# Load order at the end of attention, and the order of loads and forms in the output projection, of a one-core encoder block

## The chip, the cores and the metric

The kernel runs on one core of a Trainium2 chip. The metric is device time in microseconds (us) of one execution, as the median of several runs. Five engines work side by side and are ordered by semaphores: TensorE (PE in the profile; PEld is its weight load), VectorE (DVE), ScalarE (ACT), GpSimd (POOL) and SyncE (SP). SP computes nothing here: it issues nearly all DMA transfers, one behind the other, from one queue.

## The reference, cut to what matters

One residual block on x of 512 tokens by 2048 features, all in float32:

```python
h = rmsnorm(x, g_attn)
proj = h @ w_in                        # q, k, v of 8 + 8 heads of 128, and 8 forget gates
o_sb = stick_breaking_attention(...)   # 8 heads
o_fox = forgetting_attention(...)      # 8 heads
mixed = concat(head_rmsnorm(o_sb), head_rmsnorm(o_fox))
x = x + mixed @ w_out
u = relu(rmsnorm(x, g_mlp) @ w_up)
x = x + (u * u) @ w_down
y = rmsnorm(x, g_final)
```

The change touches the last head of the attention and `x + mixed @ w_out`, the output projection.

## The kernel before, in words

**Precision.** Every float32 operand of a matmul is split in two float32r parts, a high half (a cast, on ScalarE) and a low half (the operand less its high half, on VectorE). A product is three matmuls: high by high, high by low, low by high (`mm3`, lines 78 to 80). In names, `wh`, `wl` are the halves of a weight piece and `g`, `f` those of a left operand. A weight piece is 2 row blocks by 512 columns and takes 12 matmuls (2 token blocks x 2 row blocks x 3).

**The projection as seven products.** `mixed @ w_out` is computed in 2 x 2 blocks with seven block products instead of eight (numbered 1, 5, 6, 3, 7, 4 and 2), once for each of two column halves, `db` 0 and 1. Each product p needs a left *form* of the blocks of mixed: `a_source` (line 1329) makes it with one subtraction or addition on VectorE for 5, 6, 7 and 3, in place, so that the form of 6 is built on that of 5 and that of 3 on that of 6. `g_form(p, (m0, m1), ...)` (line 1498) makes the forms for row blocks m0 to m1 and splits them (cast on ScalarE, low half on VectorE). The right sides are sums of blocks of w_out that were made and stored in device memory during the attention (`wsums`, `whigh`, `wraws`).

**Product 2 comes early.** It needs only heads that are finished early (the forgetting heads). So its four pieces for each column half stand in the schedule of the attention's last step, n = 16, at the time `t` = 16 steps. The class `Second` (line 1136 on) loads a piece (`load_parts` for half 0, both halves from `wraws`, line 1146; `load` for half 1, raw), and multiplies it. The pieces go in the order m0 = 4, 6, 0, 2. The pieces 4, 6 and 0 take the next tiles of a ring of three (`hi_lo`, line 69); piece 2 has tiles of its own.

**Who sets the order.** In the attention a `Plan` collects jobs with times and emits them sorted by time. TensorE, ScalarE and VectorE run them in exactly that order. For SP this holds only up to the job `free_loads` (line 1280); behind that a planner orders SP's transfers by a simulation of its own, in which an earlier place in the program means a higher priority. In the output projection no order is written by hand: the planner places all engines, and `tc.issue_after(ins)` only says that what is traced inside it must come behind `ins` on the engine of `ins`.

**The transpose.** The weights of each head but the last are turned by a DMA: `halves` (ScalarE copies the 16-bit halves apart, line 941) at 24.7 us of a step and `turn_halves` (line 945, a `dma_start_transpose` on SP) at 24.8 us. The steps are 26.05 us long, so for head 14 these stand at t - 1.35 and t - 1.25 of step 16. The turned weights are joined (line 949), split (`ph` line 953, `pl` line 956) and multiplied with v (`product` of head 14, output tile `o`).

**The loop of the projection** (line 1623) goes over the products and the four pieces m0 = 0, 2, 4, 6 of each. `out_piece` loads, splits and multiplies a piece and returns the load. Behind a piece the loop may
- turn a finished quarter of the residual stream (`turn_quarter`, line 1567: eight transposes on TensorE into two PSUM buffers, four scaled copies on ScalarE into the tile `hr[db][j]`, and a store); column half 1 uses the same buffers for `hr[1][j]` as half 0 for `hr[0][j]`,
- make one pending left form for the up projection (`left_form`, line 1588) from `hr[0][j]`, behind the last cast and the last low half so far,
- begin a quarter (`begin`, line 1543: a load of x of 512 KB), to which `take` (line 1547) adds the product,
- make forms of mixed for a later product (the table `G_AT`, line 1594).

Piece (6, 4) means m0 = 4 of product 6.

Of the kernel before, what the change touches and what calls it, by code (L numbers as in the profile page):

```python
# [38 lines left out]
def block_kernel(ctx, tc, x, g_attn, w_in, b_f, g_out_sb, g_out_fox, w_out, g_mlp, w_up, w_down, g_final, y):  # L39
# [16 lines left out]
    lows, last_heads = [None], [None] * 7  # L56
# [165 lines left out]
    with ExitStack() as stage:  # L222
# [23 lines left out]
        plan = Plan()  # L246
# [82 lines left out]
        for k in range(2, K8):  # L329
            if k < 6:  # L330
                room[k] = early_w[0][:, 4:6] if k == 2 else early_w[1][:, 2 * k - 6:2 * k - 4]
                w = Placed(room[k])
            else:
                w = Piece(w_rows[k][:, :, c0:c0 + m], 2, m)
# [41 lines left out]
        for k in range(4, K8):  # L376
            t, j = mm_at[k], k + K8
            w = pieces[k][0]
# [387 lines left out]
    with tc.tile_pool(name="att", bufs=1, side="right", reuse_waits="tile") as at, \  # L766
# [9 lines left out]
        plan = Plan()  # L776
# [403 lines left out]
        for n in range(2 * NH + 1):  # L1180
            t = TPER * n
# [33 lines left out]
            else:  # L1215
# [4 lines left out]
                for db in range(2):  # L1220
                    for n0, m0 in enumerate((4, 6, 0, 2)):
                        w = Second(db, m0)
                        if db:
                            plan.at(t + (-10.0, -9.0, -8.0, 6.0)[n0], w.load)
                            plan.at(t + (3.4, 4.5, 10.3, 11.35)[n0], w.cast_apart if n0 < 2 else w.cast, *((n0,) if n0 < 2 else ()))
                            plan.at(t + (4.6, 7.0, 11.75, 12.95)[n0], w.low)
                        else:
                            plan.at(t + (-11.0, -5.5, 0.1, -1.4)[n0], w.load_parts)
                        for tt in range(2):
                            plan.at(t + at_unit16(unit), w.multiply, tt)  # L1230
                            unit += 1
# [266 lines left out]
    def g_form(p, *parts):  # L1498
        for m0, m1 in parts:
            a_form(p, mixed_halves[:, m0:m1], [g[:, m0:m1, :] for g in G[p]])  # L1500
# [90 lines left out]
        a_form(p, hr[db][j], [F[p][db][:, 2 * j:2 * j + 2, c, :] for c in range(2)])  # L1591

    pending, to_turn = [], []
    G_AT = {(5, 6): (3, (0, 4), (4, 6)), (6, 0): (3, (6, 8)), (6, 2): (7, (0, 4)), (6, 4): (7, (4, 6)), (6, 6): (7, (6, 8))}
    for db in range(2):
        quarter[0, 0] = second_x[db]
        if db == 1:
            pending += [(1, 0, j) for j in (1, 0)]
        else:

            g_form(1, (0, 4), (4, 6))
            with tc.issue_after(last_heads[2].ins):
                g_form(4, (0, 4), (4, 8))
            with tc.issue_after(last_heads[5].ins):
                g_form(5, (0, 4), (4, 6))
            more_parts.append(lambda: parts_at(px, "px"))
            with tc.issue_after(last_heads[3].ins):
                out_piece(1, 0, 0)
            with tc.issue_after(last_heads[0].ins):
                out_piece(1, 0, 2)  # L1610
                out_piece(1, 0, 4)
            begin(1, 0, 0)
            with tc.issue_after(last_heads[1].ins):
                for m0 in (0, 2, 4, 6):
                    ins = out_piece(4, 0, m0)
            for p in (1, 5):
                g_form(p, (6, 7), (7, 8))
            take(4, 0)
            with tc.issue_after(ins.ins):
                begin(1, 1, 0)  # L1620
            with tc.issue_after(last_heads[6].ins):
                g_form(6, (0, 4), (4, 6), (6, 8))
        for p in (1, 5, 6, 3, 7, 4)[:6 if db else 5]:
            for m0 in () if db == 0 and p == 1 else (0, 2, 4, 6):
                if db == 0 and p == 5 and m0 == 6:
                    out_piece(1, 0, 6)
                    take(1, 0)
                    last_heads[4] = taken[0]
                    to_turn += [(0, 0, 0)]
                ins = out_piece(p, db, m0)  # L1630
                if m0 in (0, 2) and to_turn:
                    with tc.issue_after(ins.ins):
                        turn_quarter(*to_turn.pop(0))
                    if db == 1 and p == 4:
                        left_form(1, 1, 1)
                        for j in range(2):
                            left_form(2, 1, j)
                        for q in (4, 5, 6):
                            left_form(q, 1, 1)
                if pending:  # L1640

                    with tc.issue_after(casts[0].ins), tc.issue_after(lows[0].ins):
                        left_form(*pending.pop(0))
                if (db or p in (3, 7, 4)) and m0 in (2, 6) and first_loads:

                    with tc.issue_after(ins.ins):
                        u, k, a = first_loads.pop(0)
                        units[u].load(k, a)
                if db == 0 and p == 5 and m0 == 6:

                    with tc.issue_after(ins.ins):
                        begin(0, 1, db)
                if db == 0 and (p, m0) in G_AT:

                    with tc.issue_after(last_heads[4].ins):
                        g_form(*G_AT[p, m0])
            if db == 0 and p == 6:
                more_parts.pop()
                px_cm.__exit__(None, None, None)
# [8 lines left out]
            if db == 1 or p != 1:  # L1668
                take(p, db)
            if db == 1:  # L1670
                pending += [(q, 0, j) for j in range(2) for q in {1: (4, 5, 6), 6: (2, 7, 3)}.get(p, ())]
            if len(squares) > 0:

                with ExitStack() as order_:
# [596 lines left out]
```

## Time and profile before

| | |
|---|---|
| median of 3 runs | 2011.31 us (2009.68 to 2012.33) |
| the profiled execution, its own time | 2010.09 us |
| its span, from the first to the last instruction | 2008.3 us |
| granted TensorE clock over the span | 0.998 |
| TensorE busy | 1992.1 us |
| VectorE busy | 1754.1 us |
| ScalarE busy | 1204.9 us |
| GpSimd busy | 63.4 us |

How to read the profile. A line of the timeline gives the start and the length in us, the engine, the line of the kernel, the operation, output<-inputs, the shape, and the count of merged instructions. In brackets stands how long the engine was idle before it and what ended that. `SPq` lines are transfers being issued on SP's queue: their length is the issue, not the transfer. A matmul's length is its latency; they follow each other sooner than that. A row of the waits gives who waited for whom, the total in us, how often, and the longest. A row of windows gives the stretch, its length, busy time of PE, PEld, DVE, ACT and POOL with counts, the granted clock, the mean share of the DMA engines and GB/s.

By stage, from windows of 20 us: TensorE is busy for all of nearly every window. It is short of 20 us from 580 to 600 (15.58), 640 to 660 (18.77), 660 to 680 (19.69), 720 to 740 (19.66), 760 to 780 (18.90), 780 to 800 (19.95), and at the end, from 2000 on. The last step of the attention begins at about 585, the output projection lies between about 614 and 757, the up projection begins at 757.

### The profile page before, as it was taken

To read this page: it belongs to the slowest core of one execution; us is meant where nothing else is said; L and a number is where in the kernel's file an instruction comes from. 1 tells how busy PE (TensorE), PEld (TensorE's weight loads), DVE (VectorE), ACT (ScalarE), POOL (GpSimd) and SP (SyncE) were. 2 spreads that over 40 slices of the span, in tenths; PEclk is the share of its full clock that TensorE was granted. 3 is DMA by queue.
4 is the path that set the end of the run, shared out by engine and by line. 5 is a ranking of instruction groups with operands and counts; after the bars stand their busy time and mean duration, and the time that the engine had idled before them with its cause. 6 is when DMAs were issued, how large, how long until landed. Compare 5 with 4: busy or idle time off the path is not lost.

```text
span 2008.3 us, 26668 instructions
## 1 busy us (share of the span) xinstructions
PE 1992.1 (99%) x10096; PEld 1709.8 (85%) x10096; DVE 1754.1 (87%) x1992; ACT 1204.9 (60%) x1636; POOL 63.4 (3%) x73
## 2 busy tenths in 40 slices
PE   9999999999999999999999999999999999999998
PEld 9988888888878789888888888888888888888887
DVE  8876888888887688999999999998798888988896
ACT  7544666677874565767676766766543444444444
POOL 0000011111010000000000000000000000000003
PEclk9999999999999999999999999999999999999999
DMA  7336977677786872566666665666795674674642
GB/s 263 125 139 212 283 240 238 201 218 231 225 264 230 305 238 95 182 206 208 204 189 215 190 222 189 210 202 234 251 328 173 234 269 154 234 268 166 215 164 85
DMA packets 309072, 426.66 MB, mean 212 GB/s; under 512 B 49440, under 2 KB 198736, under 8 KB 302416
## 3 DMA queue, kind: packets, MB, share of 16 engines
q1 hardware_dynamic: 307920, 422.33, 63.7%
q10 hardware_dynamic: 1024, 2.63, 0.3%
q8 instruction: 79, 1.29, 0.2%
q14 instruction: 49, 0.40, 0.1%
HBM read 318.07 MB, written 97.01 MB: 207 GB/s over the span
## 4 chain that ended last, share of the span: by engine, by line
PE 95%; DVE 2%; DMA 1%; ACT 1%; issue 0%; DVEq 0%; SPq 0%; ACTq 0%
PE psa L1415 11%; PE accd L80 8%; PE accd L78 8%; PE accd L79 8%; PE accq L78 6%; PE accq L80 6%; PE accq L79 6%; PE psa L1413 6%; PE psc L1415 5%; PE psc L1413 3%; PE psb L1415 3%; PE psb L1413 1%; PE m L80 1%; PE m L78 1%; PE m L79 1%; PE vy L79 1%
## 5 line engine op out<-in xcount | busy, mean ns | idle before, releaser
L2057 ACT CAST wh<-wd 128x1024 fp32r<-128x1024 f32 x126 | 124.9, 998 | 168.8 <-PE accd L80 54.6
L1943 DVE TENSOR_TENSOR wl<-wu,wh 128x1024 fp32r<-128x1024 f32 x157 | 191.4, 1220 | 13.5 <-ACT wh L1937 13.4
L78 PE MATMUL accq<-hH,wh 128*128 128x512 f32 x512 | 200.3, 391 | 0.0
L79 PE MATMUL accq<-hL,wh 128*128 128x512 f32 x512 | 199.4, 389 | 0.0
L80 PE MATMUL accq<-hH,wl 128*128 128x512 f32 x512 | 199.3, 389 | 0.0
L1937 ACT CAST wh<-wu 128x1024 fp32r<-128x1024 f32 x157 | 166.4, 1060 | 48.7 <-PE psc L1415 25.7
L1415 PE MATMUL psa<-f,wh 128*128 128x512 f32 x712 | 177.1, 391 | 0.0
L79 PE MATMUL accd<-wl,uf 128*128 128x512 f32 x436 | 169.6, 389 | 0.0
L80 PE MATMUL accd<-wh,uf 128*128 128x512 f32 x436 | 169.6, 389 | 0.0
L78 PE MATMUL accd<-wh,uf 128*128 128x512 f32 x436 | 169.4, 389 | 0.0
L2064 DVE TENSOR_TENSOR wl<-wd,wh 128x1024 fp32r<-128x1024 f32 x126 | 144.0, 1152 | 11.5 <-ACT wh L2057 11.5
L1415 PEld LDWEIGHTS psa<-f,wh 128*128 128x128 f32 x712 | 130.8, 188 | 25.3
L2057 ACT CAST wx<-wd 128x1024 fp32r<-128x1024 f32 (+1 forms) x82 | 80.8, 995 | 106.8 <-PE accd L80 42.9
L1778 DVE TENSOR_TENSOR m<-m,accd 128x1024 f32<-128x1024 f32 x84 | 102.2, 1217 | 46.7 <-PE accd L80 46.7
L80 PEld LDWEIGHTS accq<-hH,wl 128*128 128x128 f32 x512 | 96.1, 188 | 20.3
L78 PEld LDWEIGHTS accq<-hH,wh 128*128 128x128 f32 x512 | 96.2, 188 | 19.0
L79 PEld LDWEIGHTS accq<-hL,wh 128*128 128x128 f32 x512 | 96.2, 188 | 18.9
L78 PE MATMUL accd<-wx,uf 128*128 128x512 f32 x284 | 110.5, 389 | 0.0
L79 PE MATMUL accd<-wx,uf 128*128 128x512 f32 x284 | 110.5, 389 | 0.0
L80 PE MATMUL accd<-wx,uf 128*128 128x512 f32 x284 | 110.5, 389 | 0.0
L1413 PEld LDWEIGHTS psa<-f,wl 128*128 128x128 f32 x712 | 94.8, 191 | 5.2
L1413 PE MATMUL psa<-f,wl 128*128 128x256 f32 x712 | 97.2, 282 | 0.0
(498 smaller groups left out, 5072.4 us busy)
## 6 DMA issues: line engine op xcount, KB each, us to landing
wu<-in_w_up_dram SPq DMA_DIRECT2D x60, 1024.0 KB, 6.6
ufd<-st SPq DMA_DIRECT2D x98, 512.0 KB, 3.6
wd<-in_w_down_dram SPq DMA_DIRECT2D x48, 1024.0 KB, 8.1
uf<-ufd SPq DMA_DIRECT2D x42, 1024.0 KB, 6.6
wraw<-in_w_in_dram SPq DMA_DIRECT2D x64, 512.0 KB, 5.8
wo<-wsums SPq DMA_DIRECT2D x28, 512.0 KB, 5.1
wd<-in_w_down_dram SPq DMA_DIRECT2D x16, 768.0 KB, 8.0
uf<-ufd SPq DMA_DIRECT2D x14, 768.0 KB, 4.5
```

The source lines that it names most:

```text
L78: pe.matmul(out, sh, mh, start=first, stop=False, skip_group_check=True)
L79: pe.matmul(out, sh, ml, start=False, stop=False, skip_group_check=True)
L80: return pe.matmul(out, sl, mh, start=False, stop=last, skip_group_check=True)
L1413: ins = pe.matmul(ps[:, 2 * P:], lo[:, a, :], f_parts(p, a)[0], start=False, stop=last, skip_group_check=True)
L1415: ins = pe.matmul(ps, hi[:, a, :], f_both(p, a), start=a == PAIRS[0] and p in (1, 5), stop=last, skip_group_check=True)
L1778: dve.tensor_tensor(M[p][:, :, db, :], M[p][:, :, db, :], ps, op=ALU.add)
L1937: act.copy(rooms[k][0], srcs[k])
L1943: lows[0] = dve.tensor_tensor(lo, srcs.pop(k), hi.bitcast(F32), op=ALU.subtract)
L2057: act.copy(rooms[k + 3][0], srcs[k + 3])
L2064: dve.tensor_tensor(rooms[k + 2][1], srcs.pop(k + 2), rooms[k + 2][0].bitcast(F32), op=ALU.subtract)
```

## The change

It has five edits; none adds or removes an instruction.

1. In step 16 the four early loads of product 2 for column half 0 have the plan times -11.0, -5.5, 0.1 and -1.4 (pieces 4, 6, 0, 2). They become -11.0, -5.5, -1.4 and -1.35: piece 0 now stands ahead of piece 2, and both ahead of the transpose of head 14 (-1.25).
2. Forms of mixed: the last part of form 6 (row blocks 6 and 7) is no longer made before the loop but behind piece (5, 6); form 3 stays where it was; the first part of form 7 moves from (6, 2) to (6, 0), and its other parts from (6, 4) and (6, 6) to (3, 0), behind the latest low half.
3. Loads around product 6: the load of piece (3, 2) must come behind the load of piece (6, 4), and the load of x for quarter (0, 1) (`begin(0, 1, db)`) moves from behind (5, 6) to behind (6, 4).
4. In column half 1 the turn that waits in product 7 comes behind piece m0 = 2 instead of m0 = 0.
5. The pending left forms of half 0 go product by product, j = 0 and 1 of each, instead of all products for j = 0 and then for j = 1.

```diff
-                            plan.at(t + (-11.0, -5.5, 0.1, -1.4)[n0], w.load_parts)
+                            plan.at(t + (-11.0, -5.5, -1.4, -1.35)[n0], w.load_parts)
...
-    G_AT = {(5, 6): (3, (0, 4), (4, 6)), (6, 0): (3, (6, 8)), (6, 2): (7, (0, 4)), (6, 4): (7, (4, 6)), (6, 6): (7, (6, 8))}
+    G_AT = {(5, 6): ((6, (6, 8)), (3, (0, 4), (4, 6))), (6, 0): ((3, (6, 8)), (7, (0, 4))), (3, 0): ((7, (4, 6), (6, 8)),)}
...
-                g_form(6, (0, 4), (4, 6), (6, 8))
+                g_form(6, (0, 4), (4, 6))
...
-                ins = out_piece(p, db, m0)
-                if m0 in (0, 2) and to_turn:
+                with ExitStack() as order_:
+                    if db == 0 and p == 3 and m0 == 2:
+                        order_.enter_context(tc.issue_after(behind.ins))
+                    ins = out_piece(p, db, m0)
+                if m0 in ((2, 4) if db and p == 7 else (0, 2)) and to_turn:
...
-                if db == 0 and p == 5 and m0 == 6:
+                if db == 0 and p == 6 and m0 == 4:
+                    behind = ins
 
                     with tc.issue_after(ins.ins):
                         begin(0, 1, db)
                 if db == 0 and (p, m0) in G_AT:
 
-                    with tc.issue_after(last_heads[4].ins):
-                        g_form(*G_AT[p, m0])
+                    for form_ in G_AT[p, m0]:
+                        with tc.issue_after((lows[0] if p == 3 else last_heads[4]).ins):
+                            g_form(*form_)
...
-                pending += [(q, 0, j) for j in range(2) for q in {1: (4, 5, 6), 6: (2, 7, 3)}.get(p, ())]
+                pending += [(q, 0, j) for q in {1: (4, 5, 6), 6: (2, 7, 3)}.get(p, ()) for j in range(2)]
```

`last_heads[4]` is the addition of product 1 to its quarter, `lows[0]` the latest low half.

## The prediction

> **What bounds the kernel now.** I read the page first, then the list of waits of TensorE, then the timeline at the longest of them.
>
> ```profile
> span 2008.3 us, 26668 instructions
> ...
> PE 1992.1 (99%) x10096; PEld 1709.8 (85%) x10096; DVE 1754.1 (87%) x1992; ACT 1204.9 (60%) x1636; POOL 63.4 (3%) x73
> ...
> PE 95%; DVE 2%; DMA 1%; ACT 1%; issue 0%; DVEq 0%; SPq 0%; ACTq 0%
> ```
>
> TensorE is busy for 99% of the span and is 95% of the chain that ended last. The change removes no matmul, so it can only win what TensorE spends waiting or running slowly. The waits are few:
>
> ```profile
> PE acc L79 <- DMA wl<-wraws: 3.7, 1, 3.7
> ...
> PE accoa L78 <- DMA wh<-whigh: 0.9, 1, 0.9
> PE acc L78 <- ACT w L873: 0.8, 1, 0.8
> PE psc L79 <- DVE f L1828: 0.7, 1, 0.7
> ...
> PE tr L1559 <- DVE x L1552: 0.3, 1, 0.3
> PE accoc L79 <- DVE wl L61: 0.3, 1, 0.3
> PE tr L1559 <- ACT hr L1565: 0.3, 1, 0.3
> ```
>
> The first and third rows are one place, the beginning of the early piece m0=0 of product 2 (column half 0). Its timeline, then two windows of it (columns: stretch, PE, PEld, DVE, ACT, POOL, granted clock, DMA share, GB/s):
>
> ```profile
> 588.39 0.39 PE L80 MATMUL acc<-wh,g2l 128*128 128x512 f32 x1
> 589.53 0.47 PE L78 MATMUL acc<-wh,g 128*128 128x512 f32 x1 [0.75 <-ACT w L873]
> 593.67 0.64 PE L79 MATMUL acc<-wl,g 128*128 128x512 f32 x1 [3.67 <-DMA wl<-wraws]
> 594.11 0.63 PE L80 MATMUL acc<-wh,g 128*128 128x512 f32 x1
> ...
> 597.65 0.39 PE L80 MATMUL acc<-wh,g 128*128 128x512 f32 x1
> 597.88 0.39 PE L78 MATMUL acc<-w,g 128*128 128x512 f32 x1
> ```
>
> ```profile
> 593.67:597.40 3.73, 3.73 (x9) 2.96 (x10) 2.32 (x3) 2.34 (x2) 1.69 (x2) 0.54 0.54 211
> 597.88:600.60 2.72, 2.72 (x14) 2.25 (x12) 2.72 (x4) 2.72 (x3) 0.00 (x0) 1.00 0.52 133
> ```
>
> One piece (12 matmuls) takes 2.72 us when nothing holds it: that is the second window, the piece m0=2. Matmuls follow each other by 0.23 (597.65 to 597.88), so after the one at 588.39 the piece could have begun at 588.62 and the next one at 588.62 + 2.72 = 591.34. It began at 597.88. **The place costs 6.54 us**, not the 3.7 that the list shows: 0.9 for the high half wh, 3.9 for the low half wl, and 1.7 because the granted clock was 0.54 for 3.73 us behind the pause (3.73 x 0.46).
>
> **Part 1: the load order.** What kept wl is in the timeline of SP's queue:
>
> ```profile
> 581.32 0.98 SPq L1146 DMA_DIRECT2D w<-wraws  x2
> 582.35 0.42 SPq L1146 DMA_DIRECT2D wh<-wraws  x1
> 582.95 6.72 SPq L945 DMA_TRANSPOSE pl<-pt  x1
> 589.72 0.57 SPq L1146 DMA_DIRECT2D wl<-wraws  x1
> 590.38 0.38 SPq L166 DMA_DIRECT2D wraw<-in_w_out_dram  x1
> ```
>
> The queue gave out both halves of m0=2 (w, needed last), then wh of m0=0, and was then held by the transpose of head 14 for 6.72 us. The change gives the four in the order wh, wl, w, w, all wanted by the plan ahead of the transpose. What they cost is still 4 issues of 0.4 to 0.6 us; the transpose begins some 0.4 later. When do they land?
>
> ```profile
> DMA to landing us min/median/max: 7.7/7.8/7.9
> ```
>
> ```profile
> 581.30:588.60 7.30, 7.30 (x36) 6.02 (x35) 6.83 (x10) 6.01 (x7) 0.00 (x0) 1.00 0.93 251
> ```
>
> The first row is for the loads of this line whose landing is recorded. It bounds the two halves of m0=0 from above: 581.32 + 7.9 = 589.2 and 581.73 + 7.9 = 589.6, at most 1 us behind 588.62. From below: two loads of 0.524 MB at the 251 GB/s of the window are 4.2 us from 581.3, so 585.5, and nothing waits. I take nothing, since the load now third (wh, 582.35) let its matmul start at 589.53 and those ahead of it must land sooner. The "ACT w L873" of that row is only the event that came last; the matmul reads wh and g. The w halves become third and fourth: 589.5, and 2.1 us of transfer (0.524 MB at 251 GB/s) later, 591.6; they are needed at 591.34 and 591.57. I count nothing, with 0.3 as the upper bound.
>
> So TensorE arrives 6.54 us earlier at what follows. **What is late next:** the product of head 14, in the hand-written order of TensorE. Its operand pl comes over a chain that the change does not shorten:
>
> ```profile
> 595.06 1.04 ACT L173 CAST wh<-wraw 128x1024 fp32r<-128x1024 f32 x1 [2.11 <-issue]
> ...
> 599.92 1.26 ACT L953 CAST ph<-pt 128x1280 fp32r<-128x1280 f32 x1
> ```
>
> ```profile
> 596.14 1.23 DVE L180 TENSOR_TENSOR wl<-wraw,wh 128x1024 fp32r<-128x1024 f32 x1 [1.41 <-ACT wh L173]
> 597.28 2.96 DVE L886 TENSOR_TENSOR_SCAN w<-w 128x128 f32<-128x128 f32 x4
> ...
> 601.28 1.49 DVE L887 TENSOR_TENSOR w<-s,w 128x1280 f32<-128x1280 f32 x1
> 602.68 1.48 DVE L956 TENSOR_TENSOR pl<-pt,ph 128x1280 fp32r<-128x1280 f32 x1
> ```
>
> ```profile
> 608.76 0.28 PE L78 MATMUL o<-ph,vh 128*128 128x256 f32 x1
> 608.87 0.28 PE L79 MATMUL o<-pl,vh 128*128 128x256 f32 x1
> ```
>
> ```profile
> wraw<-in_w_out_dram SPq DMA_DIRECT2D x1, 512.0 KB, 4.6
> ```
>
> wraw, the last raw piece of column half 1, is issued at 590.38 and lands 4.6 us later, at 594.98; ScalarE casts it at once (595.06), and VectorE goes from 596.14 without a pause to 604.16, when pl is ready. TensorE would want pl at 608.87 - 6.54 = 602.33. It waits 1.9 us (1.83 and a little for the signal). What the chain does itself: one load less stands between the transpose and wraw (590.38 - 589.72 = 0.7 earlier), one more stands ahead of the transpose (2.1 later at most). The bytes ahead of wraw are the same as before, so I take 0, with -0.7 and +2.1 as ends. **Gain of part 1: 6.54 - 1.9 = 4.6**, from 5.3 down to 6.54 - 4.0 = 2.5 by these ends.
>
> Does the pause of 1.9 us halve the clock again? That of 3.67 did; that of 0.9 on wh<-whigh did not (clock 1.00 in the window quoted in part 2). If 1.9 us did, 1.7 more would be lost and the gain of part 1 would be 2.9; I take that it doesn't, being nearer to 0.9. The Trainium skill ("TensorE: Matmul & The Clock Gate", Part 1: The HAM clock gate) says that the clock halves after a whole idle window of about 3.4 us; by that rule the sum stays as it is, and no row here lies between 0.9 and 3.67 to test it.
>
> Head 15's chain leaves room (its exponentials wait for TensorE now), and the output projection behind it is fed by loads that wait for buffers which TensorE and VectorE free, so I let it shift as a whole.
>
> **Part 2: around product 6.** No instruction is added or dropped. One load of x and one of a product-3 piece move behind the load of piece m0=4 of product 6, and forms of 6, 3 and 7 (a subtraction, a cast and a subtraction each) move to later places.
>
> ```profile
> 637.71 2.93 SPq L1545 DMA_DIRECT2D x<-in_x_dram  x3
> ```
>
> ```profile
> wh<-whigh SPq DMA_DIRECT2D x1, 512.0 KB, 10.3
> ```
>
> ```profile
> 642.00:661.50 19.50, 17.98 (x82) 14.05 (x80) 16.53 (x22) 9.85 (x19) 0.00 (x0) 1.00 0.96 369
> ```
>
> The second row is the load of product 6's second piece, 10.3 us in a queue that is 96% busy; TensorE waits 0.9 for it. Each load moved behind it takes 0.524 MB / 369 GB/s = 1.4 us off its queue, so one of the two is enough: gain 0.9. Their cover: the moved x is added only to the finished sums of product 6, and the moved piece belongs to the product behind it. VectorE's late low half (0.3) and late addition (0.3) may go as well, since forms leave its queue; other waits may come. Ends: 0.9 + 0.6 = 1.5, and -0.5 if the later forms push another low half. I take 0.9.
>
> **Part 3: turns and left forms of half 1.** Same instructions, other order.
>
> ```profile
> 739.16 1.39 PE L1559 MATMUL tr<-ident,x 128*128 128x128 f32 x8 [0.26 <-ACT hr L1565]
> ```
>
> ```profile
> 720.00:740.00 20.00, 19.66 (x89) 15.85 (x88) 20.00 (x25) 13.44 (x21) 0.00 (x0) 1.00 0.75 228
> ```
>
> The turn in product 7 goes one piece later, 2.72 us; that covers the 0.26. But its transposes need the buffers of an earlier turn, and that one writes the first hr tile only when the last form of the old hr tile is made; that one (product 3, j = 0) goes from third to fifth among the six left forms, two pieces or 5.44 us later. VectorE is full here (20.00 of 20), so what is asked first is not what is done first. Ends: +0.3 and 0.26 - (5.44 - 2.72) = -2.5. I take 0, the row's own small wait.
>
> **Sum:** 4.6 + 0.9 + 0 = 5.5 us. The profiled execution took 2010.09 us, 1.8 around its span of 2008.3, and would take 2004.6. It is 1.2 below the median of the runs, 2011.31; that median becomes **2005.8 us**. A measurement of this kernel tells about 0.2%, 4.0 us, from no change; the sum is beyond it by 1.5.
>
> **Rivals.**
> - *The transpose is pushed back.* Its issue took 6.72 us:
>
> ```profile
> L945 SPq DMA_TRANSPOSE pl<-pt x15: 2484/2557/6717, 216.4 to 583.0; - x15
> ```
>
> The other transposes take 2.6, so this one already stands behind the loads. If a fourth load delays it and wraw by the whole 2.1, TensorE waits 4.0 at head 14, longer than the pause that halved the clock, and 1.7 is lost again: gain 6.54 - 4.0 - 1.7 + 0.9 = 1.7, 2009.6. Against it: wl no longer stands ahead of wraw. Chance 0.14. The Trainium skill ("DMA: Bandwidth & Descriptors", Queues, rings and completion order) says that each DMA engine takes descriptors in ring order, which speaks against the change in this way; the 6.72 agrees.
> - *The order isn't what the plan asks.* SP is not under the hand-written order here: the planner gave out wh (plan 0.1) ahead of the transpose (-1.25) and wl behind it. If wl stays behind, only part 2 is left: 2011.31 - 0.9 = 2010.4. Chance 0.06.
> - *The gain comes back in the projection.* VectorE's full stretch meets a TensorE that is earlier by more than VectorE is, by 2 us or more: 2007.8 to 2009. Chance 0.12.
> - *Slower.* The freed hr tile decides: at three turns of half 1 TensorE waits 2.7 us for transposes' buffers, and one long pause halves the clock: 3 x 2.72 + 1.7 = 9.9 against 5.5, so 2015.7. It decides from 5.5 us of waits at turns on; now there are 0.3. Chance 0.06.
>
> **Numbers.** The forecast has 0.62. Faster by over 0.2% (below 2007.3) takes the forecast, 0.62; within takes the first three rivals, 0.32; slower the last, 0.06. The range goes from both parts at their better ends (5.3 + 1.5 + 0.3 = 7.1, 2004.2, less 1 us of scatter between runs, 2003.2) to the case where only part 2 works, 2010.4.
>
> **What would show it.** Right: four loads of line 1146 ahead of the transpose; no wait on wraws and no window of clock 0.5 near 594; the list of waits has a new row at head 14's product, "o", for pl, of 1 to 2.5 us; no wait on whigh. Wrong: wl still behind the transpose; the wait at "o" above 3 with a low clock behind it; a wait of over 1 us at "tr" after 735 or at "accoc" in product 3.

## The result and the profile after

The changed kernel takes 2003.68 us (median of 6 runs, 2002.29 to 2004.66) against 2011.67 for the kernel before beside it: ratio 0.9961, 95% interval 0.9948 to 0.9974. That is faster by 8.0 us, or 0.39%, more than the 0.2% that this measurement can tell. The forecast was 5.5 us (2005.8), so the direction is right and the time lies inside the range; 2.5 us more were won than the sum said.

First the page's head and chain, then the list of waits of TensorE:

```profile
span 2000.6 us, 26669 instructions
...
PE 1989.1 (99%) x10096; PEld 1708.7 (85%) x10096; DVE 1754.5 (88%) x1992; ACT 1205.0 (60%) x1636; POOL 63.1 (3%) x73
...
PE 97%; DMA 1%; DVE 1%; issue 0%; ACT 0%; SPq 0%; DVEq 0%; ACTq 0%
```

```profile
PE vx L306 <- DVE still L302: 1.6, 1, 1.6
PE o L79 <- DVE pl L956: 1.5, 1, 1.5
PE tr L1559 <- ACT hr L1565: 0.6, 1, 0.6
PE accoa L78 <- DMA wx<-whigh: 0.3, 1, 0.3
PE tr L266 <- DMA xa<-in_x_dram: 0.3, 1, 0.3
```

The waits on wraws are gone, and a new one stands at head 14's product ("o"). The wait of 0.9 on whigh, which was for `wh`, product 6's second piece, is gone too; the 0.3 on whigh in this list is another, for `wx`, its fourth. But the row on `psc` (0.7), which the prediction quoted, and one on `psb` (0.4), which it left out, are gone as well, and no step of the sum had priced them.

Where the time went is best seen between matmuls that both kernels have, five of each: the last of the input projection, the last of head 14's product, the first of column half 1, the last of the output projection, and one in the up projection behind which the two run in step. Before, then after:

```profile
581.12 0.39 PE L80 MATMUL accq<-hH,wl 128*128 128x512 f32 x1
...
610.52 0.27 PE L80 MATMUL o<-ph,vl 128*128 128x128 f32 x1
...
686.80 0.39 PE L78 MATMUL accob<-wh,g 128*128 128x512 f32 x1
...
757.19 0.39 PE L80 MATMUL accoc<-wh,g 128*128 128x512 f32 x1
...
783.48 0.28 PE L79 MATMUL psa<-f,wh 128*128 128x256 f32 x1
```

```profile
581.53 0.39 PE L80 MATMUL accq<-hH,wl 128*128 128x512 f32 x1
...
606.16 0.27 PE L80 MATMUL o<-ph,vl 128*128 128x128 f32 x1
...
680.70 0.39 PE L78 MATMUL accob<-wh,g 128*128 128x512 f32 x1
...
751.33 0.39 PE L80 MATMUL accoc<-wh,g 128*128 128x512 f32 x1
...
775.70 0.28 PE L79 MATMUL psa<-f,wh 128*128 128x256 f32 x1
```

The differences of neighbours give four stages, which are used for all kernels below:

| stage | before | after | gain | forecast |
|---|---|---|---|---|
| S1, to head 14's product | 29.40 | 24.63 | 4.77 | 4.6 |
| S2, column half 0 with product 6 | 76.28 | 74.54 | 1.74 | 0.9 |
| S3, column half 1 with the turns | 70.39 | 70.63 | -0.24 | 0 |
| S4, start of the up projection | 26.29 | 24.37 | 1.92 | not in the sum |

Together 8.19; the 0.41 that the execution after was late at the first of these matmuls (its start waited 0.3 for xa) makes it 7.78, and behind the last of them the two do not move against each other.

**S1 in the profile.** SP's queue, then TensorE at the beginnings of the pieces m0=0 and m0=2 and at head 14:

```profile
581.72 0.32 SPq L1146 DMA_DIRECT2D wh<-wraws  x1
582.13 0.71 SPq L1146 DMA_DIRECT2D wl<-wraws  x1
582.90 0.90 SPq L1146 DMA_DIRECT2D w<-wraws  x2
583.90 6.81 SPq L945 DMA_TRANSPOSE pl<-pt  x1
590.81 0.52 SPq L166 DMA_DIRECT2D wraw<-in_w_out_dram  x1
```

```profile
589.02 0.39 PE L78 MATMUL acc<-wh,g 128*128 128x512 f32 x1
...
591.74 0.39 PE L78 MATMUL acc<-w,g 128*128 128x512 f32 x1
...
604.41 0.39 PE L79 MATMUL o<-pl,vh 128*128 128x256 f32 x1 [1.51 <-DVE pl L956]
```

All four loads stand ahead of the transpose, both pieces begin on time (2.72 us apart, no bracket), and the time saved is stopped at head 14, where TensorE waits 1.51 for pl. VectorE's queue shows why pl is late:

```profile
596.33 1.23 DVE L180 TENSOR_TENSOR wl<-wraw,wh 128x1024 fp32r<-128x1024 f32 x1 [1.18 <-ACT wh L173]
597.47 2.97 DVE L886 TENSOR_TENSOR_SCAN w<-w 128x128 f32<-128x128 f32 x4
...
602.87 1.48 DVE L956 TENSOR_TENSOR pl<-pt,ph 128x1280 fp32r<-128x1280 f32 x1
```

It idles 1.18 us for the cast of the last raw piece, and everything behind that, pl included, comes in order.

**S4 in the profile.** VectorE at the start of the up projection, before and after:

```profile
764.32 0.68 DVE L1337 TENSOR_TENSOR hr<-hr 128x512 f32<-128x512 f32 x1
765.69 0.69 DVE L61 TENSOR_TENSOR f<-hr,f 128x512 fp32r<-128x512 f32 x1 [0.69 <-ACT f L60]
766.90 2.36 DVE L1844 TENSOR_TENSOR wl<-wu,wh 128x1024 fp32r<-128x1024 f32 x2 [0.52 <-ACT wh L1841]
```

```profile
756.20 0.69 DVE L1337 TENSOR_TENSOR hr<-hr 128x512 f32<-128x512 f32 x1
...
758.55 1.22 DVE L1849 TENSOR_TENSOR wl<-wu,wh 128x1024 fp32r<-128x1024 f32 x1
759.68 0.68 DVE L61 TENSOR_TENSOR f<-hr,f 128x512 fp32r<-128x512 f32 x1
```

Before, the subtraction (L1337), its cast on ScalarE and the low half f follow at once, VectorE idles 0.69 and 0.52 us behind the cast, and both wl wait in line. After, the subtraction comes 4.9 us behind the last matmul of the projection instead of 7.1 (756.20 - 751.33, 764.32 - 757.19), one wl stands ahead of f, and there is no idle time. None of the edits names these instructions: the planner places them.

### The profile page after: what moved, and what is told of

Its sections match the earlier page's. It is cut to its first block, busy times and chain, and to the rows that moved or that the text cites. A ratio compares the mean times of both kernels' runs of the same rounds, so it can differ in the third digit from the quotient of the medians.

```text
span 2000.6 us, 26669 instructions
## 1 busy us (share of the span) xinstructions
PE 1989.1 (99%) x10096; PEld 1708.7 (85%) x10096; DVE 1754.5 (88%) x1992; ACT 1205.0 (60%) x1636; POOL 63.1 (3%) x73
## 4 chain that ended last, share of the span: by engine, by line
PE 97%; DMA 1%; DVE 1%; issue 0%; ACT 0%; SPq 0%; DVEq 0%; ACTq 0%
PE psa L1415 11%; PE accd L79 8%; PE accd L80 8%; PE accd L78 8%; PE accq L78 6%; PE accq L79 6%; PE accq L80 6%; PE psa L1413 6%; PE psc L1415 5%; PE psc L1413 3%; PE psb L1415 3%; PE psb L1413 1%; PE m L79 1%; PE m L78 1%; PE m L80 1%; PE vy L79 1%
## 5 line engine op out<-in xcount | busy, mean ns | idle before, releaser
L1415 PEld LDWEIGHTS psa<-f,wh 128*128 128x128 f32 x712 | 130.8, 188 | 25.3
```

Of the source, the lines that this page charges most:

```text
L1415: ins = pe.matmul(ps, hi[:, a, :], f_both(p, a), start=a == PAIRS[0] and p in (1, 5), stop=last, skip_group_check=True)
```

## The experiments

Each was timed in 5 rounds beside the kernel before. The first four take the change apart and try the wait at head 14.

**Edit 1 alone** (e1).

```diff
-                            plan.at(t + (-11.0, -5.5, 0.1, -1.4)[n0], w.load_parts)
+                            plan.at(t + (-11.0, -5.5, -1.4, -1.35)[n0], w.load_parts)
```

> The kernel before with edit 1 alone (the load order of product 2's early pieces). The traces of before and after put 4.8 us of the gain before 610 us, 1.7 around product 6 and 1.7 at the start of the up projection. Theory: each gain belongs to its own edits, so this kernel gains 4.8 us (about 2006.9), all of it by head 14's product, with a wait of about 1.5 on pl there, and the later stalls of the kernel before (0.9 on whigh, 0.7 on f in the up projection) are still in its list of waits. Rival: the gain in the up projection comes from TensorE being earlier against VectorE or against the planner's clock, whatever the left forms do; then this kernel gains 6.5 us (about 2005.2) and the stall on f is gone. Second rival: the order alone does little and the rest of the change frees the queue; then it gains under 3 us.

Measured: 2005.23 us, ratio 0.9969 (0.9956 to 0.9981). Two rows of its waits:

```profile
PE o L79 <- DVE pl L956: 2.5, 1, 2.5
...
PE tr L1559 <- DVE x L1552: 1.4, 1, 1.4
```

S1 is 25.61, a gain of 3.8; S2 is 77.42, a loss of 1.1, with a wait of 1.4 for x at the first turn. That it comes of TensorE being earlier isn't shown: e3 and e5 below, without edit 1, wait 0.9 and 1.1 there. And the stall of S4 is gone (24.87). So the theory that each gain has its own edits fell at once, and the first rival was right about S4. On VectorE the order of this kernel differs from that of the kernel before in one thing: in the up projection one wl has passed f.

**Edits 2 and 3 alone** (e2).

```diff
-    G_AT = {(5, 6): (3, (0, 4), (4, 6)), (6, 0): (3, (6, 8)), (6, 2): (7, (0, 4)), (6, 4): (7, (4, 6)), (6, 6): (7, (6, 8))}
+    G_AT = {(5, 6): ((6, (6, 8)), (3, (0, 4), (4, 6))), (6, 0): ((3, (6, 8)), (7, (0, 4))), (3, 0): ((7, (4, 6), (6, 8)),)}
...
+                    if db == 0 and p == 3 and m0 == 2:
+                        order_.enter_context(tc.issue_after(behind.ins))
...
-                if db == 0 and p == 5 and m0 == 6:
+                if db == 0 and p == 6 and m0 == 4:
+                    behind = ins
```

> The kernel before with edits 2 and 3 alone (forms of 6, 3 and 7, and the loads around product 6). Theory: the gain around product 6 belongs to these edits: 1.7 us (about 2010.0), the wait of 0.9 on whigh at 655 is gone or under 0.4, and so are those at 650.5 and 661.5 (0.3 each). Rival, as the prediction had it: only the wait on whigh goes, 0.9 us. Rival from the shift: product 6 is only undisturbed because everything came 4.4 us earlier; then this kernel gains nothing there. At 594 it still has the wait of 3.7 on wl.

Measured: 2009.02 us, ratio 0.9985 (0.9977 to 0.9994). S2 is 74.58, 1.70 less than before; the waits at the first turn, in product 3 and on whigh for product 6's second piece are gone, and one of 0.3 on whigh for its fourth piece (`wx`) has come. S4 is 24.89: again without the stall, again with wl ahead of f.

**Edits 4 and 5 alone** (e3).

```diff
-                if m0 in (0, 2) and to_turn:
+                if m0 in ((2, 4) if db and p == 7 else (0, 2)) and to_turn:
...
-                pending += [(q, 0, j) for j in range(2) for q in {1: (4, 5, 6), 6: (2, 7, 3)}.get(p, ())]
+                pending += [(q, 0, j) for q in {1: (4, 5, 6), 6: (2, 7, 3)}.get(p, ()) for j in range(2)]
```

> The kernel before with edits 4 and 5 alone (the turn in product 7 one piece later, the left forms product by product). Theory: the gain at the start of the up projection belongs to these edits: 1.7 us in all (about 2010.0): the waits of 0.4 on wl and 0.7 on f between 768 and 775 are gone, the wait at the turn of product 7 is 0.6 instead of 0.3. Rival: these edits do nothing for the time, or lose the 0.3 at the turn, and the up projection starts better only because of the shift by the other edits: 0 to +0.3 us (2011.3 to 2012), with the waits on wl and f still there.

Measured: 2010.18 us, ratio 0.9993 (0.9985 to 1.0002), so not told from no change. Its profile: S4 24.37 (1.92 gained), S3 71.04 (0.65 lost; the turn waits 1.0), S2 76.95 with the old loads and forms.

**The low half of the last raw piece behind the scans** (e4: the changed kernel and one number).

```diff
-                            plan.at(t + (4.6, 7.0, 11.75, 12.95)[n0], w.low)
+                            plan.at(t + (4.6, 7.0, 11.75, 14.6)[n0], w.low)
```

> The changed kernel with one more edit: the low half of the last raw piece of column half 1 has the plan time 14.6 instead of 12.95, so on VectorE it comes behind the scans of the last head instead of ahead of them. Theory: the wait of 1.5 us at head 14's product is VectorE's order: the scans stand behind a low half that waits for a load until 596.3, while VectorE is idle for 1.2 us before it, so the scans start 1.2 to 2 us earlier and pl is ready about 1.0 to 1.4 us earlier: the wait falls to 0.1 to 0.5 and the kernel gains about 1.0 us (2002.7). Rival: pl waits for ph (ScalarE, ready at 601.4), not for VectorE; then at best pl starts at 601.4, which also gives up to 1.4, but if ph itself comes later the wait stays at 1.5. Rival that loses: the low half, now 3 us later, is late for piece m0=2 of column half 1, which wants it at 601.5: a new wait of up to 0.5 at acc, and the gain is 0.5 or less.

Measured: 2002.54 us, ratio 0.9956 (0.9942 to 0.9969). The wait for pl is 0.9 and S1 24.07, 0.56 less than after: in the theory's direction, half of its size, since the join of the turned halves on ScalarE still stood behind the cast of that raw piece.

**The exchange in the up projection alone** (e5: the kernel before, with none of the change's edits). The left form is taken out of the projection's loop and given three plan times. ScalarE's order stays as it was.

```diff
-                        for q in (4, 5, 6):
+                        for q in (4, 5):
                             left_form(q, 1, 1)
...
-    for p, j, total, cast, low in ((7, 1, None, -1.0, 1.5), (4, 0, None, 5.95, 7.1), (5, 0, 7.8, 8.45, 9.7), (6, 0, 14.1, 14.85, 16.0),
+    for p, j, total, cast, low in ((7, 1, None, -1.0, 1.5), (6, 1, -0.5, 0.05, 3.5), (4, 0, None, 5.95, 7.1), (5, 0, 7.8, 8.45, 9.7), (6, 0, 14.1, 14.85, 16.0),
```

> The kernel before with none of the change's edits; instead one left form of the up projection (product 6, j = 1 of column half 1) is placed by hand. On VectorE this puts its subtraction two places forward and its low half f behind the low half wl that it stood ahead of; nothing else moves there. Each of the runs of one part alone had that exchange of f and wl too, made by the planner, and each lost the stall at the start of the up projection. Theory: the exchange by itself is worth what they gained there, 1.4 to 1.9 us: VectorE no longer idles 0.7 + 0.5 us behind f's cast, the waits on wl (0.4) and f (0.7) go, median about 2010.0. Rival: the stall went because TensorE and VectorE met in another phase, and the exchange alone gives under 0.4.

Measured: 2010.05 us, ratio 0.9993 (0.9984 to 1.0002); S4 25.25, a gain of 1.04. The time alone can't tell it from no change, the stage can. It is three quarters of the theory's lower end: a wait of 0.3 on f stayed. This run moves two things, the subtraction forward and f behind wl, and doesn't tell them apart.

**Without edits 4 and 5** (e6: the changed kernel with these lines as before).

```diff
-                if m0 in ((2, 4) if db and p == 7 else (0, 2)) and to_turn:
+                if m0 in (0, 2) and to_turn:
...
-                pending += [(q, 0, j) for q in {1: (4, 5, 6), 6: (2, 7, 3)}.get(p, ()) for j in range(2)]
+                pending += [(q, 0, j) for j in range(2) for q in {1: (4, 5, 6), 6: (2, 7, 3)}.get(p, ())]
```

> The changed kernel without edits 4 and 5, so edits 1, 2 and 3. Here the planner puts f ahead of wl again, as in the kernel before, and their subtraction where it was. Theory (the exchange makes the stall): the waits of 0.4 on wl and 0.7 on f are back, 1.4 us are lost at the start of the up projection, and up to 0.3 is won at the turn of product 7: about 2004.8. Rival (the stall belongs to the phase, or to nothing in VectorE's order): the waits stay away, 2003.7 or 0.3 better. If edits 4 and 5 are worth something by themselves, through the earlier subtraction, it is the same 1.4.

Measured: 2006.35 us, ratio 0.9973 (0.9962 to 0.9984). Two rows of its waits:

```profile
PE psc L79 <- DVE f L1833: 0.7, 1, 0.7
...
PE psb L80 <- DVE wl L1849: 0.4, 1, 0.4
```

S4 is 26.28, the stall of the kernel before to a hundredth, in a kernel that is otherwise earlier than it by 3 us. So the stall doesn't go with the phase. Nor does it go with the order of f and wl alone: in e8 (below) f stands ahead of both wl again, and S4 is 24.34 all the same. Two rows of VectorE in e8:

```profile
757.67 0.69 DVE L1337 TENSOR_TENSOR hr<-hr 128x512 f32<-128x512 f32 x1
...
760.02 0.69 DVE L61 TENSOR_TENSOR f<-hr,f 128x512 fp32r<-128x512 f32 x1
```

There the subtraction stands two instructions further ahead of f, so that ScalarE casts while VectorE works, and nothing idles. What makes the stall is f directly behind its own subtraction, with the cast between them. Putting f behind a wl (e1, e2) or the subtraction further ahead (e8) each removes it; the other kernels with edit 5 have both. The median of e6 lies 1.5 above the theory's 2004.8; in the profiled execution S1 was 27.53, for a reason that belongs to the clock (last section).

**Without edit 2** (e7, the first pair of lines) and **without edit 3** (e8, the rest), each otherwise the changed kernel.

```diff
-    G_AT = {(5, 6): ((6, (6, 8)), (3, (0, 4), (4, 6))), (6, 0): ((3, (6, 8)), (7, (0, 4))), (3, 0): ((7, (4, 6), (6, 8)),)}
+    G_AT = {(5, 6): (3, (0, 4), (4, 6)), (6, 0): (3, (6, 8)), (6, 2): (7, (0, 4)), (6, 4): (7, (4, 6)), (6, 6): (7, (6, 8))}
...
-                    if db == 0 and p == 3 and m0 == 2:
-                        order_.enter_context(tc.issue_after(behind.ins))
...
-                if db == 0 and p == 6 and m0 == 4:
-                    behind = ins
+                if db == 0 and p == 5 and m0 == 6:
```

> The changed kernel without edit 2 (the forms of 6, 3 and 7 at their old places), with all the rest. On VectorE the addition of product 1 to x then stands behind the subtractions of the forms again. The run of edit 1 alone waited 1.4 us at the first turn for that x, 1.1 more than the kernel before, so part of what the load order gained was given back there. Theory: edit 2 is what keeps it; without it the wait at the first turn is 1.0 to 1.5 and the kernel loses 1.0 to 1.4 (about 2004.9). Rival: the loads (edit 3) do it all, and this kernel is within 0.4 us of the changed one.

> The changed kernel without edit 3 (the load of x and that of piece (3, 2) at their old places), with all the rest. Theory, by the prediction: the wait on whigh at product 6 is back, 0.6 to 0.9 instead of 0.3, and 0.3 to 0.6 us are lost; up to 0.4 more at the start of the up projection, where f stands ahead of wl but its cast is early (about 2004.4). Rival: the loads cost nothing to TensorE where they were, once it arrives earlier: within 0.2 us of the changed kernel. Rival on the other side: TensorE, now earlier against a full queue, waits more than in the kernel before, 1.5 us or more at product 6 (2005 or above).

Measured: 2004.79 us, ratio 0.9967 (0.9954 to 0.9979), and 2005.43 us, ratio 0.9972 (0.9960 to 0.9984). In S2 they are nearly alike, 75.27 and 75.36. Without edit 2 no wait for x came back at the first turn, against the expectation; a wait of 0.6 for a low half in product 3 did. Without edit 3 the wait of 0.8 on whigh for the second piece came back, as expected. Over all kernels S2 is 76.28 to 77.42 with neither edit (before, e1, e3, e5; mean 76.9), 75.3 with one, and 74.54 to 75.61 with both (eight executions, mean 75.0). So either edit brings some 1.6 us; what the second adds, 0.3, is less than those eight differ among themselves. They are not two terms to be added.

Why one is enough to remove the wait for x is in the traces. Times in this paragraph are counted from the last matmul of head 14's product. With neither edit VectorE makes the addition that the turn waits for at 38.7 to 39.8 us, and the turn follows it at once (40.0 to 41.1). With edit 2 alone it is made at 37.2, since two instructions of form 6 (L1337, L61) no longer stand ahead of it, and the turn at 39.5 finds it done. With edit 3 alone it is made at 37.9, and the planner has put the turn one piece later, at 42.2.

The loads themselves win little. Product 6 loads whigh four times. Edit 3 takes the moved loads away from ahead of the second of them and puts them ahead of the fourth, which goes to the tile `wx`. SP's queue in the changed kernel, then the fourth load from issue to landing, before and after:

```profile
643.98 0.42 SPq L1545 DMA_DIRECT2D x<-in_x_dram  x1
...
646.66 0.92 SPq L1515 DMA_DIRECT2D wx<-whigh  x1
```

```profile
wx<-whigh SPq DMA_DIRECT2D x1, 512.0 KB, 9.4
```

```profile
wx<-whigh SPq DMA_DIRECT2D x1, 512.0 KB, 11.4
```

In the five kernels without edit 3 the fourth load takes 9.0 to 9.7 us, and TensorE waits 0.6 to 0.9 for the second. In the nine executions with it the fourth takes 11.4 to 12.8, and TensorE waits there instead, 0.1 to 1.2 us (0.3 in the execution after, 1.2 when the same kernel ran again, e0). So the loads moved the wait. What S2 wins is for the most part the wait for x (0.3 to 1.4, mean 0.9, with neither edit) and that for the low half in product 3 (0.3 to 0.6); with both edits neither wait is left.

**The changed kernel again, and its chain taken apart** (e0, e9).

> The changed kernel once more, unaltered, beside the next two. In the runs with edit 1 the transpose's issue took 6.8 to 8.4 us and the wait at head 14's product was 1.5 to 2.6 us, with the same instructions up to there. Theory: that is scatter of the transfers from execution to execution, so this one lies in the same span (wait 1.5 to 2.6, median 2003 to 2005). Rival: the order of later loads differs between those kernels and makes it; then this execution shows 6.8 and 1.5 again.

Measured: 2004.05 us, ratio 0.9961 (0.9949 to 0.9974); the transpose's issue took 6.77 and the wait for pl 1.4. So the rival was nearer here: two executions of this kernel agree, and the longer issues (7.4 to 8.4) were in other kernels. But edits 2 to 5 touch nothing ahead of the transpose, so what stretches it in those is open.

```diff
-                            plan.at(t + (3.4, 4.5, 10.3, 11.35)[n0], w.cast_apart if n0 < 2 else w.cast, *((n0,) if n0 < 2 else ()))
-                            plan.at(t + (4.6, 7.0, 11.75, 12.95)[n0], w.low)
+                            plan.at(t + (3.4, 4.5, 10.3, 12.45)[n0], w.cast_apart if n0 < 2 else w.cast, *((n0,) if n0 < 2 else ()))
+                            plan.at(t + (4.6, 7.0, 11.75, 14.6)[n0], w.low)
...
-                for dt, f in zip((12.4, 15.5, 19.3) if last_ else (5.4, 8.5, 9.8), (H.join_halves, H.t_high, H.t_low)):
+                for dt, f in zip((12.4, 14.65, 14.7) if last_ else (5.4, 8.5, 9.8), (H.join_halves, H.t_high, H.t_low)):
...
-                    ins = out_piece(4, 0, m0)
+                    with tc.issue_after(last_heads[7].ins), tc.issue_after(last_heads[8].ins):
+                        ins = out_piece(4, 0, m0)
```

Here `last_heads[7]` and `[8]` are head 14's ph and pl.

> The changed kernel with head 14's chain taken from behind the last raw piece: ScalarE joins the turned halves ahead of that piece's cast (12.4 before 12.45 instead of behind 11.35), VectorE does the scans and the subtraction of the last head ahead of its low half (14.6 instead of 12.95), and pl follows (14.7), with the first early piece of product 4 put behind ph and pl. Theory: the wait of 1.5 to 2.6 us at head 14's product comes from this order of ScalarE and VectorE, not from the transpose; pl is ready at about 602 instead of 604.4 and later, the wait is gone or under 0.5, the place returns all of its 6.5 us instead of 4.8, and the kernel gains 1.0 to 2.2 us more: about 2002.0. Rival: the transpose lands so late (594 and after in the slow executions) that join, ph and pl end at 603 or later whatever the order: gain 0.5 or less. Rival that loses: the low half of the last raw piece or the first piece of product 4 is late instead, 0.5 us or more at acc or accob, and the turn of the last head waits.

Measured: 2001.64 us, ratio 0.9949 (0.9936 to 0.9961), 2.4 below the changed kernel beside it. ScalarE and VectorE at head 14:

```profile
593.33 3.12 ACT L949 COPY pt<-pl 128x2560 uint16<-128x2560 uint16 x1
596.30 1.05 ACT L173 CAST wh<-wraw 128x1024 fp32r<-128x1024 f32 x1
597.25 1.26 ACT L953 CAST ph<-pt 128x1280 fp32r<-128x1280 f32 x1
```

```profile
595.38 3.15 DVE L886 TENSOR_TENSOR_SCAN w<-w 128x128 f32<-128x128 f32 x4 [0.30 <-POOL w L837]
...
599.98 1.21 DVE L180 TENSOR_TENSOR wl<-wraw,wh 128x1024 fp32r<-128x1024 f32 x1
601.11 1.48 DVE L956 TENSOR_TENSOR pl<-pt,ph 128x1280 fp32r<-128x1280 f32 x1
```

pl is ready at 602.6, the wait is gone, and S1 is 22.92: 6.48 less than before. That is nearly the whole cost of the place, which the prediction had put at 6.54, and it came in spite of a transpose of 7.4 us.

**The turn of product 7: edit 4 or edit 5** (e10: e9 with the first pair of these lines; e11: e9 with the second, and the left form placed by hand as in e5).

```diff
-                if m0 in ((2, 4) if db and p == 7 else (0, 2)) and to_turn:
+                if m0 in (0, 2) and to_turn:
...
-                pending += [(q, 0, j) for q in {1: (4, 5, 6), 6: (2, 7, 3)}.get(p, ()) for j in range(2)]
+                pending += [(q, 0, j) for j in range(2) for q in {1: (4, 5, 6), 6: (2, 7, 3)}.get(p, ())]
```

> The kernel of the run above without edit 4, so that the turn in product 7 stays behind its first piece. The kernels with edits 4 and 5 waited 0.5 to 1.0 us at that turn for hr, the kernel before 0.3, and the one without both 0.2 or less. Theory: edit 4 makes that wait, since it puts the turn's copies among ScalarE's casts of the last pieces; without it the wait is 0.3 or less and 0.3 to 0.7 us are won (about 2001.5). Rival: edit 5 makes it, the freed hr tile coming two forms later, and then this kernel waits more, 1 us or over.

> The kernel with the chain reordered, without edit 5 (the left forms go by j again, as before) but with edit 4; the exchange of f and wl at the start of the up projection is placed by hand, as in the run of the exchange alone. The run without edit 4 still waited 1.0 us at the turn of product 7, so edit 4 is not the cause. Theory: edit 5 is: it frees the hr tile two forms later. Without it the turn waits 0.3 or less, 0.7 to 1.0 us are won there, the stall of the up projection stays away (1.0 to 1.4 won of it instead of 1.9), and the kernel takes 2000.8 to 2001.5. Rival: the two edits each make a part of it, or it is scatter of the loads that ScalarE's casts wait for; then 0.6 or more stays.

Measured: 2001.08 us, ratio 0.9947 (0.9933 to 0.9960), and 2001.90 us, ratio 0.9955 (0.9941 to 0.9968). Without edit 4 the turn still waited 1.0; without edit 5 no row for it is left in the list of waits. The stretch from the middle of column half 1 (its 145th matmul) to its last is 34.41 to 35.00 us in the six kernels without edit 5 (mean 34.6) and 34.57 to 35.78 in the eight executions with it (mean 35.4): edit 5 costs about 0.8 us there, edit 4 nothing. One kernel with edit 5 stands apart: e8 has 34.57 and no wait at the turn. How edit 5 makes the wait isn't shown. ScalarE at that turn in the execution after:

```profile
731.74 1.05 ACT L60 CAST wh<-wo 128x1024 fp32r<-128x1024 f32 x1 [1.68 <-DMA wo<-wsums]
732.70 1.56 ACT L1565 ACTIVATE hr<-tr,g_rest 128x256 f32<-128x256 f32 x4
```

The copies that free the turn's buffers (L1565) began without idle time, right behind a cast that had idled 1.68 us for a load. So ScalarE did not stand still for the hr tile; it stood still for that load. In S4 edit 5 gives 24.34 to 24.39, the exchange by the planner 24.9, by hand 25.3. So the two ways end alike, and e9, e10 and e11 can't be told apart by their times. All three lie below both kernels.

## Why the prediction was right, and where its sum was off

The time lies inside the range by 0.5 us and with some luck: the better ends of both parts gave 2004.2, and only the 1 us that was allowed for scatter covers 2003.68. The main step held; two of its smaller terms came about in other ways than the prediction said.

**What bounds the kernel, and the place at 588.** Right. Nearly all of the 6.54 us was there to be had (6.48 in e9), the halved clock went with the pause, and the bounds on the landings held: "I take nothing" for the four loads was 0 in this trace (in one other execution, e8, wl was 0.7 late, inside the bound of 1).

**What is late next.** Right: the new wait is at "o", for pl, 1.51 in this execution against 1.9, and 1.4 to 2.6 in all executions with edit 1 and the old chain; the chain's own shift, taken as 0 with ends -0.7 and +2.1, was between 0 and 1.8 (pl began at 602.68 before and at 602.65 to 604.44 in those). The gain of part 1 is 4.77 against 4.6, and 4.8 again in e0; in e1, e7 and e8, with longer issues of the transpose, it was 3.0 to 3.8, and in e6, with the halved clock, 1.9. That the clock would not halve for such a wait was right here. The prediction found no row between 0.9 and 3.67 us to test it; the list before has one, 1.6 us on vx at the start of the kernel, and the clock behind it, from 13.00 to 16.50, was 1.00. The chain named was the right one, but its cause was read too narrowly: not the landing of wraw alone, but that three things which don't need it stood behind its cast in hand-written order.

**Part 2 came out larger, and not by its own step.** The term "gain 0.9" was 1.74 here, 1.9 in the mean, and 0.8 in e0. The step was that the loads moved behind product 6's third load cover themselves. The wait that it counted went, but the moved loads then stood ahead of the fourth load of whigh, and TensorE waited there, 0.3 us here and 0.7 in the mean of the eight executions with both edits, against 0.7 at the second load in the mean of the four with neither. That fourth load was left out. "No wait on whigh", one of the signs of being right, did not come true. In the queue three loads had moved, not two: that of piece (3, 4) followed. Whether one of them would do, as the prediction has it, no run shows. What was won are the waits for x and for the low half in product 3 (0.3 each), put into the upper end as 0.6; they were larger in other executions (0.9 to 1.4 for x in e1, e3 and e5).

**Part 3 failed as a step.** "I take 0, the row's own small wait", with ends +0.3 and -2.5. S3 lost 0.24 here and 0.8 in the mean, by edit 5, which is the direction of the lower end; that the freed hr tile makes it, as that end had it, isn't shown (e11). But the stall at the start of the up projection, whose row on `psc` stood among the waits, was left unpriced, because no edit names its instructions. It went, and its 1.92 us put the result beyond the sum's better end. The planner sets the order of VectorE from its own simulated times, so any edit ahead of a place can turn two neighbours around in it: edit 1, edits 2 with 3, and edits 4 with 5 each did so, edits 1 to 3 together did not.

**Rivals.** The pushed-back transpose did not decide the result; a part of it is real, since in other kernels with edit 1 the issue took up to 8.4 us, and once, in e6, the long wait did halve the clock. The gain did not come back in the projection; e1's loss of 1.1 us in S2 lies within what kernels without edits 2 and 3 show there (76.3 to 77.4). The order was as planned. At the turns 0.6 us were waited, far from the 5.5 from which the slower case decides.

## What to carry to other kernels

Price a late transfer as the distance between where the work could have begun and where the next thing began, the slow clock behind the pause included; then ask which chain ends next, and look in its queues for work that doesn't belong to it. A load that is moved back stands ahead of another one: name that one, and price it too. Where a planner orders an engine's queue, every stall behind the edit is open again in both directions: list those stalls, give each its price as an end of the range, and read the orders of both kernels before believing that an edit did it. That a row of the waits has the same tensor before and after doesn't make it the same wait: compare the tile and the time. An effect of 1 us in 2000 is settled by the distance between two named instructions, in several executions, not by the median.

## What the runs showed of the hardware

**When a pause halves the clock.** Two executions with the same instructions up to there, e6 and then e7, each with one window from the end of the piece before head 14's product to its second matmul and one behind it:

```profile
602.63:605.98 3.35, 0.55 (x2) 0.19 (x2) 3.35 (x4) 3.35 (x4) 0.00 (x0) 1.00 0.59 191
605.98:609.30 3.32, 3.32 (x15) 3.32 (x16) 1.14 (x2) 0.07 (x2) 0.77 (x2) 0.56 0.78 301
```

```profile
602.63:605.77 3.14, 0.55 (x3) 0.19 (x2) 3.14 (x4) 3.14 (x4) 0.00 (x0) 1.00 0.62 197
605.77:609.10 3.33, 3.33 (x21) 3.02 (x22) 1.14 (x2) 1.33 (x4) 0.76 (x2) 1.00 0.75 301
```

A stretch of 3.35 us with one matmul in it was followed by 3.3 us at a granted clock of 0.56; one of 3.14 us was not. The single matmul did not save the clock. But the length of the pause alone does not decide. In e3, at the wait for wl of product 2's piece 0 (the place at 588), the clock fell long before TensorE had stood still that long:

```profile
588.20:591.60 3.40, 1.45 (x6) 0.65 (x4) 1.38 (x2) 2.97 (x3) 0.00 (x0) 1.00 1.31 251
591.60:595.02 3.42, 0.72 (x2) 0.62 (x3) 2.52 (x2) 1.75 (x2) 0.96 (x1) 0.50 0.93 322
595.02:598.43 3.41, 3.41 (x10) 2.64 (x9) 1.85 (x4) 2.82 (x2) 0.73 (x2) 0.50 0.31 124
```

In the 3.40 us ahead of the fall TensorE had been busy for 1.45. The clock stayed at 0.50 for 6.83 us, the last 4.1 of them with matmuls (from 594.30), and it fell at 591.60 in e5 too. The Trainium skill ("TensorE: Matmul & The Clock Gate", Part 1: The HAM clock gate) gives an idle window of about 3.4 us that runs freely, so that the point shifts with its phase. The two lengths agree with it, once (3.41 us, from 593.89, in the kernel before) and twice that window, and so does a fall in the middle of a wait; but the stretch ahead of the fall was not idle, and how much work still counts as idle no run here measures.

**The transpose behind loads.** Its issue on SP took 6.3 to 6.8 us in the four kernels without edit 1 and 6.8 to 8.4 in those with it; the wraw behind it moves by as much.
